# Layer 2's latent branch with its gates and z projections spread one by one, its merge set up two steps later, and the last column's squares summed by TensorE

## The chip, the cores and the metric

The program runs on one NeuronCore of a Trainium2 chip. The core has five engines with queues of their own: TensorE (PE; its weight loads are shown as PEld), VectorE (DVE), ScalarE (ACT), GpSimd (POOL) and SyncE (SP), which here issues every DMA. The metric is the device time of one execution in microseconds. The kernel before took 2572.04 us, the median of three runs from 2567.85 to 2572.58 us.

## The reference: what is computed

Two layers of a decoder trunk work on 16 meta tokens and 1024 tokens of width 1024. In each layer the tokens are normalised and multiplied by one wide matrix. Its columns feed three token mixers (forgetting attention, "FoX"; latent attention, "MLA"; sliding-window attention, "SWA"), one gate path z of 512 columns for each, and three times 1024 merge gates:

```python
h = rmsnorm(x, norm_g)
proj = h @ w_in          # a_q a_k a_v a_f a_z | b_cq b_ckv b_kr b_z | c_q c_k c_v c_z | gates
branches = stack([y_a * silu(a_z), y_b * silu(b_z), y_c * silu(c_z)])
proj_br = einsum('blnw,nwd->blnd', branches, w_branch)
merged = sum(sigmoid(gates) * proj_br, over the three branches)
x = x + merged @ w_out
```

A last rmsnorm closes the program, and the meta tokens are dropped. A norm needs, for each token, the sum of the squares of its 1024 values.

## The kernel before

**Tiles.** Channels lie on partitions, so a normalised input is a pair of tiles hh and hl of 128 partitions by 8 by 1040 tokens: each float32 is split into a rounded high part and the rest (split, L154). A product is then three matmuls, high by high, low by high and high by low (mm3, L171, with its three matmuls in L175 to L177). Tokens are taken in chunks: qch is two chunks of 512 in layer 2 and 264, 264 and 512 in layer 1; the last stage of layer 2 takes four of 256.

**Order of the stages in a layer.** Values and projections, then the three branches one after the other (FoX, SWA, MLA), then the merge (L1014 to L1023: for each branch n_, load_y and eight calls of branch), then the output columns with the next norm (L1026 to L1079).

**Fillers.** The attention of a head is a chain through four engines: scores on PE (L1002), a minimum on DVE (L255), an exponential on ACT (L260), transposes on PE (L268), a split by ACT and DVE (L157, L158), products with v (L310, L312). Other work stands between the groups of a head. The table PLAN (L61) has for each layer three lists, for FoX, SWA and MLA. Its entries are called in order by fill() (L737): one ahead of the branch, and one after each group of four query blocks. MLA in layer 2 has eight heads of two groups each, so 17 entries. The letters mean:

- g: gate(), L652: one of the layer's 24 merge gates is projected (8 steps of mm3 for each of two chunks, 48 matmuls), copied out by ACT (L657) and stored to gate_d;
- z: one of the branch's four z projections, also 48 matmuls, with a tanh on ACT (L734) and a product on DVE (L735) into a tile zs, of which there are two buffers; the z of head pair j is used up by POOL in L355;
- r: merge_starts(), L914: the layer's normalised input is given up (no projection may follow), its memory becomes acc and the tiles of the merge, and load_y(0) brings FoX's y from DRAM pair by pair through one buffer yt, which POOL rounds and subtracts (L936, L938);
- s: branch(0, d), L942: one of FoX's eight products with w_branch, 24 matmuls, and its gate's tanh (L952) and product (L956). What the plan leaves of the eight is done after the attention by L1022.

All fillers use the PSUM tag pj, of two banks, and the weight buffers wr, wh and wl, of two each. A weight tile is 512 KB: one DMA, a cast on ACT (L157) and a subtraction on POOL (L158).

**finish and finish_late.** After a pair of heads finish() (L322) sends the reciprocal sums through DRAM; at the end of every fill() finish_late() (L343) scales the oldest waiting pair: two products on POOL (L354 by the sums, L355 by z) and the store to y_d.

**What sets the order on an engine.** The code is traced in program order, but the program is made with schedule_with_timeline_sim=True (L1171): a planner that models the time of each instruction sets the order on each engine's queue when the program is built, within what data and buffers allow. The code's order is its priority, not the order that runs. Each queue is then served in that order.

**The norm's sum of squares.** column() (L1041) makes one of eight output columns of a chunk: mm3, the addition to x (L1044), and add_square() (L216), where ACT squares (L221) and POOL adds to the running tile sq (L222); for the last column DVE does that addition. rstd() (L187) then multiplies a matrix of ones by sq (L192), which adds over the partitions, and makes the reciprocal root (L199 to L204). This matmul is in plain float32 and appears as two records in the profile. In layer 1 the norm feeds layer 2 (normed, L207); in layer 2 it feeds the output (L1066 to L1079).

Of the kernel before, what the change touches and what calls it, by code (L numbers as in the profile page):

```python
# [11 lines left out]
F32 = mybir.dt.float32  # L12
F32R = mybir.dt.float32r
AF = mybir.ActivationFunctionType
# [4 lines left out]
P = 128  # L19
D = 1024  # L20
KD = D // P
# [42 lines left out]
     "g g . z g z g . g g zzr s . . sss s s".split()),  # L64
    ("g z . . z . g . . gg z . z g gg . gg".split(),
     "gg zg z g . gg zz g gg".split(),
     "g gg . z . z g . . g zzr . ss . ss s s".split()),
)


def _f(ap):
    return ap.bitcast(F32)
# [13 lines left out]
def tile_kernel(ctx: ExitStack, tc, a, out):  # L86
    nc = tc.nc
# [9 lines left out]
    def psum(tag):  # L97
        return ps.tile([P, 512], F32, tag=tag, name=f"ps_{tag}", bufs=PSB[tag])

    def dma(dst, src):  # L100
        nc.sync.dma_start(*(_f(x) if x.dtype == F32R else x for x in (dst, src)))
# [5 lines left out]
    def dense():  # L107

        turn[0] += 1
        return psum(banks[0][turn[0] % len(banks[0])])  # L110
# [18 lines left out]
    ones = const.tile([P, P], F32, tag="ones", name="ones")  # L129
# [24 lines left out]
    def split(hi, lo, src, scale=None, eng=None):  # L154

        if scale is None:
            nc.scalar.copy(hi, src)  # L157
            (eng or nc.vector).tensor_tensor(lo, src, _f(hi), ALU.subtract)  # L158
        else:
            nc.scalar.activation(hi, src, AF.Copy, scale=scale)  # L160
            nc.vector.scalar_tensor_tensor(lo, src, scale, _f(hi), ALU.mult, ALU.subtract)

    def weights(src, n):
        raw = wp.tile([P, 1024], F32, tag="wr", name="wr", bufs=2)
        dma(raw[:, :n], src)
        wh = wp.tile([P, 1024], F32R, tag="wh", name="wh")
        wl = wp.tile([P, 1024], F32R, tag="wl", name="wl")
        split(wh[:, :n], wl[:, :n], raw[:, :n], eng=nc.gpsimd)
        return wh, wl

    def mm3(dst, wh, wl, rh, rl, nk, m, c0, c1):  # L171

        for k in range(nk):
            w1 = wh[:, k * P:k * P + m]
            nc.tensor.matmul(dst, w1, rh[:, k, c0:c1], start=(k == 0), stop=False)  # L175
            nc.tensor.matmul(dst, w1, rl[:, k, c0:c1], start=False, stop=False)  # L176
            nc.tensor.matmul(dst, wl[:, k * P:k * P + m], rh[:, k, c0:c1],  # L177
                             start=False, stop=(k == nk - 1))
# [5 lines left out]
            mm3(t[:m, :c1 - c0], wh, wl, rh, rl, nk, m, c0, c1)  # L184
            evac(t[:, :c1 - c0], c0, c1)

    def rstd(pool, sq, c0, c1, dim, parts=None):  # L187

        n = c1 - c0
        v = psum("t")[:, :n]  # L190
        if parts is None:
            nc.tensor.matmul(v, ones, sq[:, c0:c1], start=True, stop=True)  # L192
        else:
            for k in range(parts):
                t = pool.tile([P, 512], F32, tag="sqt", name="sqt", bufs=4)[:, :n]
                nc.scalar.activation(t, sq(k)[:, c0:c1], AF.Square)
                nc.tensor.matmul(v, ones, t, start=(k == 0), stop=(k == parts - 1))
        r = pool.tile([P, 512], F32, tag="rs_r", name="rs_r", bufs=1)[:, :n]
        nc.scalar.activation(r, v, AF.Ln, bias=epsc, scale=1.0 / dim)  # L199
        nc.scalar.activation(r, r, AF.Exp, scale=-0.5)  # L200
        nc.vector.tensor_scalar(v, v, -0.5 / dim, -0.5 * EPS, ALU.mult, ALU.add)
        nc.vector.tensor_tensor(v, v, r, ALU.mult)
        nc.vector.tensor_tensor(v, v, r, ALU.mult)
        nc.vector.scalar_tensor_tensor(v, v, 1.5, r, ALU.add, ALU.mult)  # L204
        return v

    def normed(pool, xk, nk, sq, chunk, dim, gc, hh, hl, parts=None):  # L207
        c0, c1 = chunk
        r = rstd(pool, sq, c0, c1, dim, parts)
        for k in range(nk):  # L210
            h = psum("o")[:, :c1 - c0]
            nc.vector.scalar_tensor_tensor(h, xk(k)[:, c0:c1], gcol[:, gc + k:gc + k + 1], r,
                                           ALU.mult, ALU.mult)
            split(hh[:, k, c0:c1], hl[:, k, c0:c1], h)

    def add_square(pool, sq, x, c0, c1, first, eng, sqb=1):  # L216
        if first:
            nc.scalar.activation(sq[:, c0:c1], x, AF.Square)
        else:
            t = pool.tile([P, 512], F32, tag="sqt", name="sqt", bufs=sqb)[:, :c1 - c0]  # L220
            nc.scalar.activation(t, x, AF.Square)  # L221
            eng.tensor_tensor(sq[:, c0:c1], sq[:, c0:c1], t, ALU.add)  # L222
# [257 lines left out]
    def table(name):  # L480
        tc.keep_in_program_order(nc.scalar.preload_act_table_set(f"{name}_and_others"))
# [5 lines left out]
    hh = hpool.tile([P, KD, L], F32R, tag="hh", name="hh")  # L487
    hl = hpool.tile([P, KD, L], F32R, tag="hl", name="hl")
    va = tc.alloc_tile_pool(name="va0", bufs=1, side=B, reuse_waits="tile")
    banks[0] = MOST  # L490
    with tc.tile_pool(name="s0", bufs=4, side=A, reuse_waits="tile") as s0:
        x0 = s0.tile([P, KD, L], F32, tag="x0", name="x0", bufs=1)
        sq = s0.tile([P, L], F32, tag="sq", name="sq", bufs=1)
# [17 lines left out]
        for c0, c1 in START:  # L511
            xk = lambda k: x0[:, k]
# [9 lines left out]
    for l in range(DEPTH):  # L522
# [80 lines left out]
        with tc.tile_pool(name=f"wq{l}", bufs=2, side=B, reuse_waits="tile") as pw:  # L603
# [20 lines left out]
            for kv in range(2):  # L624
                ws = [weights(w1[T_CQ + 2 * kv + i], 1024) for i in range(2)]
                rows = [row_pair(pw) for _ in range(2)]
                for c0, c1 in qch:
                    n = c1 - c0
                    xs = []
                    for i in range(2):  # L630
                        t = dense()[:, :n]
# [44 lines left out]
        with tc.tile_pool(name=f"lr{l}", bufs=2, side=B, reuse_waits="tile") as pr:  # L676
            for t0, nk, dim, gc, dh, dl, chunks in (
# [3 lines left out]
                sq = pr.tile([P, L], F32, tag="sq", name="sq")  # L681
# [8 lines left out]
        with tc.tile_pool(name=f"mq{l}", bufs=2, side=A, reuse_waits="tile") as pm:  # L690
            values(vb, 1, ws, 2, cvh, cvl, between=some)
            wh, wl = weights(a["wkn"][l], 1024)
            for pair in range(4):
                rows = row_pair(pm)
                for c0, c1 in FULL:
                    t = dense()[:, :c1 - c0]
# [10 lines left out]
            for part in (2, 0, 1):  # L707
                wh, wl = weights(a["wuq"][l, part], 768)
                rows = [row_pair(pm) for _ in range(2)]
                for c0, c1 in qch:  # L710
                    n = c1 - c0
                    xs = []
                    for i in range(2):
                        t = dense()[:, :n]
# [107 lines left out]
        with tc.tile_pool(name=f"swk{l}", bufs=2, side=A, reuse_waits="tile") as pk, \  # L822
# [12 lines left out]
            for kv in range(2):  # L835
# [14 lines left out]
                for i in range(-1 if first else 0, NB):  # L850
# [11 lines left out]
                    for jj in range(2):  # L862
                        t = psum("s").rearrange("p (j c) -> p j c", j=2)
                        for j2 in range(2):
# [3 lines left out]
                                             start=True, stop=False)  # L868
                            nc.tensor.matmul(dst, ql[j][:, q0:q0 + rows], kc[:, k0:k0 + nk_],
                                             start=False, stop=True)  # L870
# [17 lines left out]
                    parts = [(0, NM, 0)] if i < 0 else [(0, P, i), (P, P, i + 1)]  # L888
                    for pi, (kcol0, kk, blk) in enumerate(parts):
# [3 lines left out]
                                         start=(pi == 0), stop=False)  # L893
                        nc.tensor.matmul(o[:, :width], vc[:kk, blk, kv, :], pl[:kk, :width],
                                         start=False, stop=(pi == len(parts) - 1))
# [134 lines left out]
        xn = xp.tile([P, KD, L], F32, tag="xn", name="xn")  # L1030
        if first:
            hpool = tc.alloc_tile_pool(name=f"h{l + 1}", bufs=1, side=A, reuse_waits="tile")
            hh = hpool.tile([P, KD, L], F32R, tag="hh", name="hh")
            hl = hpool.tile([P, KD, L], F32R, tag="hl", name="hl")
            vw = tc.alloc_tile_pool(name=f"vw{l}", bufs=1, side=A, reuse_waits="tile")
        with tc.tile_pool(name=f"so{l}", bufs=2, side=B, reuse_waits="tile") as po:
            sq = po.tile([P, L], F32, tag="sq", name="sq", bufs=1)
            for d in range(KD):
                dma(xn[:, d, lo:], (a["xT"] if first else x_d)[d][:, lo:])

            def column(d, w, c0, c1):  # L1041
                t = dense()[:, :c1 - c0]
                mm3(t, w[0], w[1], mt[c0][0], mt[c0][1], KD, P, 0, c1 - c0)
                nc.vector.tensor_tensor(xn[:, d, c0:c1], t, xn[:, d, c0:c1], ALU.add)  # L1044
                add_square(po, sq, xn[:, d, c0:c1], c0, c1, d == 0,
                           nc.vector if d == KD - 1 else nc.gpsimd, 2)
                if first:
                    dma(x_d[d, :, c0:c1], xn[:, d, c0:c1])

            for d in range(KD - 2):  # L1050
                w = weights(a["wo"][l, d], 1024)
                for c0, c1 in och:
                    column(d, w, c0, c1)
                if first and d == 2:
                    early_ws = value_weights(vw, [a["wv0"][l + 1]], KD)
            last = [(d, weights(a["wo"][l, d], 1024)) for d in (KD - 2, KD - 1)]
            banks[0] = MOST
            for c0, c1 in och:
                for d, w in last:
                    column(d, w, c0, c1)  # L1060
                if c0 == lo:
                    table("natural_log_exp")
                if first:
                    normed(po, lambda k: xn[:, k], KD, sq, (c0, c1), D, 8, hh, hl)
                else:
                    r = rstd(po, sq, c0, c1, D)  # L1066
                    rb = po.tile([P, 512], F32, tag="rb", name="rb")[:, :c1 - c0]
                    nc.scalar.copy(rb, r)
                    for k in range(KD):
                        h = xn[:, k, c0:c1]  # L1070
                        g = gcol[:, 16 + k:17 + k]
                        if k in (1, 4, 6):
                            nc.scalar.activation(h, h, AF.Copy, scale=g)
                            nc.gpsimd.tensor_tensor(h, h, rb, ALU.mult)
                        else:
                            nc.vector.scalar_tensor_tensor(h, h, g, r, ALU.mult, ALU.mult)
                        if k % 2:
                            dma(out.rearrange("k p n -> p k n")[:, k - 1:k + 1, c0 - NM:c1 - NM],
                                xn[:, k - 1:k + 1, c0:c1])  # L1079
# [6 lines left out]
            sq=3240, sk=3752, sv=3880, sz=4008, g=4520)  # L1086
# [89 lines left out]
```

## Time and profile before

| | |
|---|---|
| median of three runs | 2572.04 us (2567.85 to 2572.58) |
| the profiled execution | 2568.92 us, of which the span from its first to its last instruction is 2567.0 us |
| mean granted TensorE clock | 0.995 |
| layer 2's latent branch | from about 2093 (the first scores) to 2370 us of the span |
| layer 2's merge, rest of it | to about 2460 us |
| output columns and last norm | to 2567 us |

A row of a timeline gives the start in us from the span's start, the duration, the engine, the line, the operation, out<-in by the program's names, the shapes and how many were joined; in brackets stands the idle time before it and what ended it. Matmuls are pipelined: their ends are modelled, and the time that one costs in a dense row of them is the distance from start to start. A table by stretches gives for each engine the busy time and the number of instructions, then PE's granted clock, the busy share of the DMA engines and GB/s.

### The profile page before, as it was taken

How to read it: one execution, taken by the hardware profiler on the slowest of the kernel's cores; microseconds unless marked ns; L12 is line 12 of the kernel's file. 1: busy time of each engine (PE TensorE's matmuls, PEld its weight loads, DVE VectorE, ACT ScalarE, POOL GpSimd, SP SyncE). 2: the span in 40 equal slices, each digit the busy share in tenths (PEclk: the TensorE clock that was granted, in tenths of full speed). 3: DMA queues.
4: the chain of work that ended last, by engine and by line, in shares of the span. 5: the costliest groups of instructions: out<-in, count | busy, mean ns of one | idle time of the engine just before them, and what ended most of it. 6: DMA issues, size and time to landing. Idle time of an engine off the chain costs nothing.

```text
span 2567.0 us, 42088 instructions
## 1 busy us (share of the span) xinstructions
PE 2518.8 (98%) x15446; PEld 2252.2 (88%) x15446; DVE 1286.1 (50%) x3286; ACT 1206.4 (47%) x2704; POOL 1003.7 (39%) x983
## 2 busy tenths in 40 slices
PE   8999999999999999999999999999999999999998
PEld 7999899999888999999998888888887888888897
DVE  5464355544363445677156453545434623566743
ACT  5233355545374456654233343555445634566433
POOL 4141545344332424453523325445323342352544
PEclk9999999999999999999999999999999999999999
DMA  5144512222634434364323354121216362453532
GB/s 170 56 140 149 193 55 82 73 76 77 175 105 111 134 96 125 101 227 172 112 92 89 108 191 145 67 83 59 87 71 178 103 173 75 122 146 118 190 128 74
DMA packets 137630, 303.39 MB, mean 118 GB/s; under 512 B 22560, under 2 KB 63296, under 8 KB 137424
## 3 DMA queue, kind: packets, MB, share of 16 engines
q1 hardware_dynamic: 137424, 300.71, 37.2%
q8 instruction: 122, 2.00, 0.3%
q14 instruction: 84, 0.69, 0.1%
HBM read 211.98 MB, written 88.66 MB: 117 GB/s over the span
## 4 chain that ended last, share of the span: by engine, by line
PE 87%; DMA 5%; DVE 3%; ACT 2%; POOL 2%; issue 1%; SPq 1%; POOLq 0%; ACTq 0%; DVEq 0%
PE ps_pj L177 15%; PE ps_pj L176 15%; PE ps_pj L175 15%; PE ps_t L268 6%; PE ps_s L1002 3%; PE ps_o L312 3%; PE ps_s L176 3%; PE ps_s L177 3%; PE ps_s L175 3%; PE ps_o L310 2%; PE ps_t L177 1%; PE ps_t L176 1%; PE ps_o L176 1%; PE ps_t L175 1%; PE ps_s L804 1%; PE ps_s L802 1%
## 5 line engine op out<-in xcount | busy, mean ns | idle before, releaser
L175 PE MATMUL ps_pj<-hh,wh 128*128 128x512 f32 (+1 forms) x1920 | 673.2, 351 | 4.2 <-ACT gt L657 2.0
L158 POOL TENSOR_TENSOR wl<-wr,wh 128x1024 fp32r<-128x1024 f32 (+1 forms) x156 | 376.5, 2414 | 766.2 <-ACT wh L157 644.0
L177 PE MATMUL ps_pj<-hh,wl 128*128 128x512 f32 (+1 forms) x1920 | 670.1, 349 | 2.2 <-POOL wl L158 2.2
L176 PE MATMUL ps_pj<-hl,wh 128*128 128x512 f32 (+1 forms) x1920 | 671.5, 350 | 0.0
L175 PEld LDWEIGHTS ps_pj<-hh,wh 128*128 128x128 f32 x1920 | 361.8, 188 | 47.8 <-ACT gt L657 2.6
L177 PEld LDWEIGHTS ps_pj<-hh,wl 128*128 128x128 f32 x1920 | 362.1, 189 | 43.5 <-POOL wl L158 2.4
L176 PEld LDWEIGHTS ps_pj<-hl,wh 128*128 128x128 f32 x1920 | 361.9, 189 | 39.4 <-issue 0.5
L158 DVE TENSOR_TENSOR ptl<-ps_t,pth 128x512 fp32r<-128x512 f32 (+1 forms) x386 | 244.6, 640 | 143.1 <-ACT pth L157 137.3
L260 ACT ACTIVATE P<-P,mn 128x656 f32<-128x656 f32 (+8 forms) x272 | 207.0, 761 | 164.6 <-DVE mn L255 160.0
L157 ACT CAST pth<-ps_t 128x512 fp32r<-128x512 f32 (+1 forms) x386 | 205.8, 546 | 166.7 <-PE ps_t L268 134.7
L157 ACT CAST wh<-wr 128x1024 fp32r<-128x1024 f32 (+1 forms) x156 | 162.1, 1039 | 241.4 <-PE ps_pj L176 131.8
L268 PE MATMUL ps_t<-ident,P 128*128 128x128 f32 x1152 | 187.6, 276 | 0.8 <-DVE ptl L158 0.7
L310 PE MATMUL ps_o<-pth,vp 128*128 128x256 f32 (+1 forms) x640 | 167.5, 277 | 2.7 <-DVE u L281 1.8
L312 PE MATMUL ps_o<-ptl,vp 128*128 128x256 f32 (+1 forms) x640 | 159.5, 287 | 1.9 <-DVE ptl L158 1.7
L298 POOL COPY pmeta<-P 128x16 f32<-128x16 f32 x256 | 49.4, 196 | 271.2 <-ACT P L260 262.8
L1002 PE MATMUL ps_s<-kt,qt 96*128 96x328 f32 (+9 forms) x696 | 147.3, 329 | 2.7 <-DVE mn L255 2.7
L268 PEld LDWEIGHTS ps_t<-ident,P 128*128 128x128 f32 x1152 | 135.1, 141 | 8.9 <-DVE ptl L158 1.5
L310 PEld LDWEIGHTS ps_o<-pth,vp 128*128 128x128 f32 x640 | 121.1, 189 | 11.0 <-issue 1.7
L809 POOL TENSOR_TENSOR cm<-ckb,tri 128x128 f32<-128x128 f32 (+1 forms) x136 | 60.3, 445 | 176.4 <-DVE mn L255 172.6
L312 PEld LDWEIGHTS ps_o<-ptl,vp 128*128 128x128 f32 x640 | 120.8, 189 | 8.3 <-DVE ptl L158 4.4
L281 DVE TENSOR_TENSOR u<-ps_o,hv 64x256 f32<-64x256 f32 x128 | 53.9, 421 | 135.9 <-ACT hv L280 120.9
L1002 PEld LDWEIGHTS ps_s<-kt,qt 96*128 96x128 f32 (+1 forms) x696 | 108.9, 188 | 10.0 <-DVE mn L255 5.2
(357 smaller groups left out, 5647.3 us busy)
## 6 DMA issues: line engine op xcount, KB each, us to landing
wr<-in_w_dram SPq DMA_DIRECT2D x108, 512.0 KB
gate_d<-gt SPq DMA_DIRECT2D x72, 256.0 KB
gt<-gate_d SPq DMA_DIRECT2D x24, 520.0 KB
wr<-in_wbr_dram SPq DMA_DIRECT2D x24, 512.0 KB
gt<-gate_d SPq DMA_DIRECT2D x24, 512.0 KB
kn_d<-sg SPq DMA_DIRECT2D x16, 520.0 KB
ckb<-ck_d SPq DMA_DIRECT2D x16, 520.0 KB
kt<-kn_d SPq DMA_DIRECT2D x16, 520.0 KB
```

The costliest lines, as they stand in the source:

```text
L157: nc.scalar.copy(hi, src)
L158: (eng or nc.vector).tensor_tensor(lo, src, _f(hi), ALU.subtract)
L175: nc.tensor.matmul(dst, w1, rh[:, k, c0:c1], start=(k == 0), stop=False)
L176: nc.tensor.matmul(dst, w1, rl[:, k, c0:c1], start=False, stop=False)
L177: nc.tensor.matmul(dst, wl[:, k * P:k * P + m], rh[:, k, c0:c1], start=False, stop=(k == nk - 1))
L260: nc.scalar.activation(s[:rows, :n], s[:rows, :n], AF.Exp, bias=prev, scale=-1.0, accum_out=total)
L268: nc.tensor.transpose(t[:kk, c:c + rows], src, ident[:rows, :rows])
L281: nc.vector.tensor_tensor(u[mine, :n], o[mine, :n], t[mine, :n], ALU.add)
L310: nc.tensor.matmul(dst, vp[:, j + x, vs], ph[:, cols], start=(j + x == 0), stop=False)
L312: nc.tensor.matmul(dst, vp[:, j + x, vs], pl[:, cols], start=False, stop=(diag and x == 1))
L809: nc.gpsimd.tensor_tensor(cm[:rows, :rows], ckb[:rows, d:n], tri[:rows, :rows], ALU.add)
L1002: nc.tensor.matmul(dst, q[:, qi, q0:q0 + rows], kt[:, ki, c0:c1], start=(x == 0), stop=(x == 2))
```

## The change

Two edits that have nothing to do with each other in the code.

The third list of layer 2's plan:

```diff
-     "g gg . z . z g . . g zzr . ss . ss s s".split()),
+     "g g . z . z g . g . zg . zr . ss ss s".split()),
```

Both have 17 entries, five g, four z and one r. The second g of the second entry moves: the gates stand in entries 1, 2, 7, 9 and 11 instead of 1, 2, 2, 7 and 10. The third z stays in entry 11 and the fourth goes from entry 11 to entry 13, and r with it. The plan has five s instead of six, in entries 15, 15, 16, 16 and 17 instead of 13, 13, 15, 15, 16 and 17; so three of the eight products of FoX's merge are left for the loop after the attention, instead of two.

The squares of the last column, in both layers:

```diff
-    def rstd(pool, sq, c0, c1, dim, parts=None):
+    def rstd(pool, sq, c0, c1, dim, parts=None, more=None):
...
-            nc.tensor.matmul(v, ones, sq[:, c0:c1], start=True, stop=True)
+            nc.tensor.matmul(v, ones, sq[:, c0:c1], start=True, stop=more is None)
+            if more is not None:
+                nc.tensor.matmul(v, ones, more, start=False, stop=True)
...
-                add_square(po, sq, xn[:, d, c0:c1], c0, c1, d == 0,
-                           nc.vector if d == KD - 1 else nc.gpsimd, 2)
+                if d == KD - 1:
+                    t = po.tile([P, 512], F32, tag="sqt", name="sqt", bufs=2)[:, :c1 - c0]
+                    nc.scalar.activation(t, xn[:, d, c0:c1], AF.Square)
+                else:
+                    add_square(po, sq, xn[:, d, c0:c1], c0, c1, d == 0, nc.gpsimd, 2)
                 if first:
                     dma(x_d[d, :, c0:c1], xn[:, d, c0:c1])
+                return t
```

The squares of the last column are no longer added to sq. They stay in their own tile, column() returns it, and a second matmul with the ones adds them in PSUM to the sum that the first one makes of sq. The calls of normed() and rstd() pass the tile on as more.

More of the change, by code (lines that the diff above doesn't have):

```diff
@@ L205, in rstd, with normed @@
         return v
-    def normed(pool, xk, nk, sq, chunk, dim, gc, hh, hl, parts=None):
+    def normed(pool, xk, nk, sq, chunk, dim, gc, hh, hl, parts=None, more=None):
         c0, c1 = chunk
-        r = rstd(pool, sq, c0, c1, dim, parts)
+        r = rstd(pool, sq, c0, c1, dim, parts, more)
         for k in range(nk):
@@ L1059, in tile_kernel @@
                 for d, w in last:
-                    column(d, w, c0, c1)
+                    more = column(d, w, c0, c1)
                 if c0 == lo:
@@ L1063, in tile_kernel @@
                 if first:
-                    normed(po, lambda k: xn[:, k], KD, sq, (c0, c1), D, 8, hh, hl)
+                    normed(po, lambda k: xn[:, k], KD, sq, (c0, c1), D, 8, hh, hl, more=more)
                 else:
-                    r = rstd(po, sq, c0, c1, D)
+                    r = rstd(po, sq, c0, c1, D, more=more)
                     rb = po.tile([P, 512], F32, tag="rb", name="rb")[:, :c1 - c0]
```

## The prediction

> **What bounds the kernel now.** I read the page's busy shares first, then tables of busy time by stretch over layer 2's latent branch, then timelines at the places that they point to.
>
> ```profile
> span 2567.0 us, 42088 instructions
> PE 2518.8 (98%) x15446; PEld 2252.2 (88%) x15446; DVE 1286.1 (50%) x3286; ACT 1206.4 (47%) x2704; POOL 1003.7 (39%) x983
> ```
>
> TensorE is busy for 98% of the span. So a matmul more costs its full length wherever TensorE is full, and a rearrangement can win only idle time, 2567.0 - 2518.8 = 48.2 us in the whole program. The question is how much of that lies where the plan of layer 2's latent branch is edited. The stretches, with time, then busy time of PE, weight load, DVE, ACT and POOL, then the granted clock:
>
> ```profile
> core 0: us, PE busy (x) PEld busy (x) DVE busy (x) ACT busy (x) POOL busy (x), PEclk, DMA share, GB/s
> 2205.00:2222.00 17.00, 15.84 (x102) 14.24 (x101) 12.70 (x35) 12.95 (x29) 8.25 (x10) 0.90 0.41 89
> 2222.00:2238.00 16.00, 15.83 (x85) 13.46 (x84) 6.55 (x17) 4.90 (x11) 0.20 (x1) 1.00 0.17 56
> 2238.00:2284.00 46.00, 43.47 (x296) 38.34 (x295) 37.07 (x104) 36.60 (x80) 36.93 (x40) 1.00 0.68 184
> ...
> 2340.00:2372.00 32.00, 27.65 (x168) 23.24 (x167) 22.15 (x48) 20.26 (x42) 3.38 (x7) 1.00 0.32 109
> ```
>
> TensorE idles 17.00 - 15.84 = 1.16 us, 2.53 us and 4.35 us in three of them. I call them hole A, hole B and the end. The same table for the instructions that touch hh alone (the projections: two of three of their matmuls read it) says what the holes are:
>
> ```profile
> 2205.00:2222.00 17.00, 1.05 (x3) 0.38 (x2) 0.00 (x0) 0.00 (x0) 0.00 (x0) 0.90 0.41 89
> 2222.00:2238.00 16.00, 10.28 (x32) 6.02 (x32) 0.00 (x0) 0.00 (x0) 0.00 (x0) 1.00 0.17 56
> 2238.00:2284.00 46.00, 0.00 (x0) 0.00 (x0) 0.00 (x0) 0.00 (x0) 0.00 (x0) 1.00 0.68 184
> ```
>
> In A and B there is next to no projection to put between the attention's matmuls; all of the fourth z (32 of its 48 matmuls read hh) runs between them. What opens and closes the holes is seen in the timelines of POOL and DVE:
>
> ```profile
> 2219.30 2.40 POOL L355 TENSOR_TENSOR u<-u,zs 128x1024 f32<-128x1024 f32 x1
> ...
> 2241.34 2.95 POOL L936 TENSOR_SCALAR y<-yt 128x512 fp32r<-128x512 f32 x2
> ...
> 2280.86 2.55 POOL L938 TENSOR_TENSOR y<-yt,y 128x512 fp32r<-128x512 f32 x2
> ```
> ```profile
> 2221.73 1.28 DVE L735 SCALAR_TENSOR_TENSOR zs<-ez,ps_pj 128x512 f32<-128x512 f32 x2 [0.38 <-POOL u L355]
> ...
> 2279.01 1.28 DVE L735 SCALAR_TENSOR_TENSOR zs<-ez,ps_pj 128x512 f32<-128x512 f32 x2
> ```
>
> There are two zs buffers. The third z is multiplied but can't leave its two pj banks until POOL has used pair 0's z (L355 at 2219.30): hole A. The fourth z, multiplied by 2238, waits in the same way for pair 1's, until 2279.01. Once its matmuls are done, the layer's input is freed, the merge gets its memory, and POOL splits y from 2241.34 to 2283.4; only then has branch() operands: hole B. So the letters of the plan do not set where projections run. They run ahead, in their own order, until a buffer stops them. That decides how I price the edit.
>
> **The change, part by part.** *Order of the projections.* Before, the stream of the branch is g, g, g, z, z, g, g, z, z and then branches; after, it is g, g, z, z, g, g, z, g, z. The one real move is a gate from before the first z to between the third and the fourth. A dense projection's pitch is that of this row of the chain that ended last (start, us, what):
>
> ```profile
> 2163.66 0.23 PE ps_pj L176
> ```
>
> 48 matmuls by 0.23 us are 11.0 us for a gate, 24 by 0.23 are 5.5 us for a branch(). With the gate go its weight load and two stores on SP, ACT's cast and two copies, and POOL's 2.4 us split. All pass the loads of keys and queries on SP, and I price them at nothing: PE waits for no load in these stretches, and without the lead that those loads have one late load would cost its own few us.
>
> Before the third z there are 11.0 us less to fill with, so that z gets stuck earlier. While projections are plentiful they take some two thirds of PE (the fourth z's 11.0 us lie within 16); without them the attention speeds up, so pair 0 ends earlier too, and I let hole A grow by 8 us, not 11. Its idle rate is 1.16 / 17 = 0.07 us per us, so +0.5 us. Bounds: 0, if pair 0 ends 11 us earlier, and 2.2, with one more loss of the clock:
>
> ```profile
> 2205.00:2213.00 8.00, 6.86 (x45) 5.83 (x43) 5.49 (x16) 6.47 (x13) 2.77 (x3) 1.00 0.01 3
> 2213.00:2217.00 4.00, 3.98 (x18) 3.41 (x19) 3.55 (x10) 3.18 (x9) 0.51 (x2) 0.63 0.86 181
> ```
>
> Within hole A the granted clock is 0.63 over 4 us: half speed for 3.0 us of them, and the 0.90 of the whole 17 us makes it 17 x 0.10 x 2 = 3.4 us, a loss of 1.7 us. It came after 8 us in which PE idled 1.14 us in all. [...]
>
> *Hole B.* It runs from the last matmul of the fourth z to the end of the y split, and both ends move together. The gate that now fills after the third z shortens nothing of it; r two fills later could lengthen it, were it bound by its letter, which the trace denies. I take 0, between -2.5 (its idle gone) and +1.1 (20 us more at 2.53 / 46 = 0.055). Twenty us is a head: the exponentials of hole B are
>
> ```profile
> 2238.00:2284.00 46.00, 16.02 (x36) 1.00 0.68 184
> ```
>
> 36 records, two for each of 18 softmaxes; 8 make a head, 20.4 us.
>
> *The end.* One branch() moves from the plan to the dense loop behind it: 5.5 us more that PE can put into the end. The waits of PE there are
>
> ```profile
> PE ps_o L371 <- ACT pm L369: 1.5, 1, 1.5
> PE ps_s L175 <- ACT y L934: 1.0, 1, 1.0
> PE ps_s L176 <- POOL y L938: 0.8, 1, 0.8
> ```
>
> The last two are waits for the second branch's y, which that work can cover: -1.8 us, with -3.3 (all three) and 0 (it has run before them) as bounds. Its gate tile comes from the second pool instead of the first; I price that at nothing, since the load is issued well ahead.
>
> *Squares.* Seven DVE additions (three chunks in layer 1, four in layer 2) go, and seven matmuls on ones come. Their cost on a full PE, at 256 and at 512 columns:
>
> ```profile
> 2541.75 0.59 PE L192 MATMUL ps_t<-sq,ones 128*128 128x256 f32 x2
> 2541.99 0.47 PE L176 MATMUL ps_s<-m,wh 128*128 128x256 f32 x1
> 2542.29 0.28 PE L177 MATMUL ps_s<-m,wl 128*128 128x256 f32 x1
> 2542.41 0.28 PE L175 MATMUL ps_s<-m,wh 128*128 128x256 f32 x1
> ```
> ```profile
> 1301.41 1.02 PE L192 MATMUL ps_t<-sq,ones 128*128 128x512 f32 x2
> 1301.87 0.71 PE L456 MATMUL ps_s<-wvh,hl 128*128 128x320 f32 x1
> 1302.42 0.31 PE L454 MATMUL ps_pj<-wvh,hh 128*128 128x320 f32 x1
> 1302.56 0.31 PE L455 MATMUL ps_pj<-wvl,hh 128*128 128x320 f32 x1
> ```
>
> From 2541.75 to 2542.29 lie one such matmul and a plain one, whose pitch is 0.12: 0.54 - 0.12 = 0.42 us. At 512 columns it is 1.01 - 0.14 = 0.87 us. Layer 1 has chunks of 264, 264 and 512: 0.43 + 0.43 + 0.87 = 1.7 us. The first three chunks of layer 2 cost 3 x 0.42 = 1.3 us. Nothing hides these: PE is full there, and the additions that go were hidden behind it. Only the last chunk has the addition in its chain:
>
> ```profile
> 2554.00 0.40 ACT L221 ACTIVATE sqt<-xn 128x256 f32<-128x256 f32 x1
> 2554.39 0.43 DVE L202 TENSOR_TENSOR ps_t<-ps_t,rs_r 128x256 f32<-128x256 f32 x1
> 2554.74 0.41 DVE L222 TENSOR_TENSOR sq<-sq,sqt 128x256 f32<-128x256 f32 x1
> 2555.07 0.42 DVE L203 TENSOR_TENSOR ps_t<-ps_t,rs_r 128x256 f32<-128x256 f32 x1
> 2555.21 0.70 PE L192 MATMUL ps_t<-sq,ones 128*128 128x256 f32 x2 [1.72 <-DVE sq L222]
> ```
>
> The matmul on sq moves into PE's idle 1.72 us, the one on the squares can start at 2554.4 instead of 2555.21. But DVE has the chunk before it in hand and serves both in turn, so what reaches the end is the slot of L222 there, 2555.07 - 2554.74 = 0.3 us. I take -0.3, between 0 and -1.6 (the 0.8 us of PE's earlier start twice, should the third chunk gain it too). New is a wait on ACT: the last column's square stays in one of two buffers until its matmul has read it, so ACT's square of the next chunk may wait, with that chunk's evacuations behind it. PE's columns cover that in all chunks but the last, which has no successor.
>
> Sum: 1.7 + 1.3 - 0.3 + 0.5 + 0 - 1.8 = +1.4 us. The profiled execution took 2568.92 us, 1.9 us more than its span, and would take 2570.3. The median of the runs shown is 2572.04, 3.1 above it, which I carry over: 2573.4 us. The bounds of the terms together, -4.4 and +6.3, give 2568 to 2578. A measurement of this kernel can tell about 0.2%, 5.1 us, from no change.
>
> **The rivals.** *The holes close.* If the late gate and the late branch reach all the idle time, 1.16 + 2.53 + 4.35 us go, and with the clock drop 1.7 more: -9.7, and with the squares' +2.7 it is -7.0: 2565.0 us. For it speaks that 11.0 us of projection now lie just ahead of B; against it, that B is set by the y split, 42 us of it on POOL.
>
> *The merge really comes late.* If the two fills hold back the load of y by a head, hole B grows by 20.4 us, the clock falls once more (1.7), and the price per us decides: 0.055 as in B, or that of the end's first part, where nothing at all fills:
>
> ```profile
> 2355.00:2364.00 9.00, 6.68 (x43) 5.10 (x42) 4.82 (x9) 5.72 (x13) 0.00 (x0) 1.00 0.31 98
> ```
>
> 2.32 / 9 = 0.26. At that price it is 1.4 + 1.7 + 5.3 = +8.4: 2580.4 us. It turns the forecast into slower from 0.10 us per us on. For it: single buffers of yt, and loads of later heads queued behind them on SP. Against it: before, the merge ran well ahead of its letter.
>
> *The plan does nothing.* If the projections end up where they were, the squares' +2.7 remain: 2574.7 us.
>
> *No clock drop.* If hole A no longer has the pattern of idling that costs the clock, the sum is 1.7 lower: 2571.7 us. One drop in a trace can be chance. [...]
>
> **How the numbers follow.** Forecast 0.43, holes close 0.21, merge late 0.21, plan without effect 0.10, no drop 0.05. All but the second and third lie within 5.1 us: same 0.58, faster 0.21, slower 0.21. The three runs shown spread over 4.7 us, so 2 us go below the first rival and 0.6 above the second: 2563 to 2581. The forecast's own range is 2568 to 2578.
>
> **What would show it.** Right: fillers in the order above; hole A longer by some 8 us and B near 46; the two waits for y at the end gone; L192's neighbour with the new matmul 0.42 to 0.87 us longer in each chunk; no DVE addition of squares. Wrong: the y split starting more than 10 us after the fourth z's last matmul, TensorE idling more than 12 us between the gates and the second branch, or layer 1 changed by more than its 1.7 us.

## The result and the profile after

| | before | after |
|---|---|---|
| median | 2570.12 us (20 runs, 2566.27 to 2573.57) | 2573.78 us (20 runs, 2568.75 to 2579.39) |
| the profiled execution | 2568.92 us, span 2567.0 | 2569.45 us, span 2567.6 |

The ratio of after to before is 1.0016, with a 95% interval of 1.0009 to 1.0022: 0.0016 x 2570 = 4.1 us slower. That is within the 0.2% that the prediction called no change, and 2573.8 us lies beside the forecast of 2573.4. But the forecast set +1.4 us on a base of 2572.04; with twenty runs that base came out 1.9 us lower, and the change cost 2.7 us more than the sum said. The two nearly cancel, so it is luck that the number came so close. The question is which terms were short. The profiled execution of after is the second lowest of its 20 runs, so the spans of single profiles settle nothing here. All runs below were fast but one of 2742.24 us, of the kernel before with one s less, which its ratio leaves out.

In the changed kernel the lines behind L192 have numbers two higher, up to L1044 (before's L952 is L954). The head of its page:

```profile
span 2567.6 us, 42109 instructions
PE 2521.4 (98%) x15460; PEld 2253.0 (88%) x15460; DVE 1284.1 (50%) x3279; ACT 1207.3 (47%) x2704; POOL 1004.2 (39%) x983
```

There are 14 matmul records more (seven matmuls of two records), 7 DVE instructions less, and PE is busy 2.6 us longer. The table by stretches (time, busy PE, weight load, DVE, ACT and POOL, granted clock), with the bounds moved to where the holes now lie:

```profile
2195.00:2212.00 17.00, 15.63 (x106) 13.68 (x105) 12.82 (x36) 13.52 (x29) 8.19 (x10) 1.00 0.46 113
2212.00:2242.00 30.00, 30.00 (x165) 26.04 (x164) 11.72 (x31) 11.12 (x22) 8.10 (x6) 1.00 0.21 69
2242.00:2287.00 45.00, 41.08 (x271) 36.26 (x270) 30.82 (x87) 31.52 (x70) 31.29 (x35) 1.00 0.62 176
...
2340.00:2372.00 32.00, 29.38 (x163) 24.27 (x161) 20.17 (x45) 19.73 (x38) 5.03 (x7) 0.95 0.35 116
```

Hole A idles 17.00 - 15.63 = 1.4 us (1.2 before), hole B 3.9 us (2.5 before), the end 2.6 us (4.4 before); but the end now has a granted clock of 0.95. What opens and closes the holes is as it was. The timelines of POOL and DVE:

```profile
2208.12 2.39 POOL L357 TENSOR_TENSOR u<-u,zs 128x1024 f32<-128x1024 f32 x1
...
2249.12 2.94 POOL L938 TENSOR_SCALAR y<-yt 128x512 fp32r<-128x512 f32 x2 [0.98 <-DMA yt<-y_d]
...
2285.84 1.29 POOL L940 TENSOR_TENSOR y<-yt,y 128x512 fp32r<-128x512 f32 x1
```
```profile
2210.89 1.27 DVE L737 SCALAR_TENSOR_TENSOR zs<-ez,ps_pj 128x512 f32<-128x512 f32 x2
2272.67 1.27 DVE L737 SCALAR_TENSOR_TENSOR zs<-ez,ps_pj 128x512 f32<-128x512 f32 x2
```

The third z leaves its banks behind pair 0's L357, and the merge's products can begin only when the last split of y has ended at 2287.1, 42 us after the last matmul of a projection, which ended at 2244.7.

**What had not been foreseen lies at the end.** The products of FoX's merge leave their banks by DVE. In before, the rows of the two chunks of the first product that the plan leaves to the tail (d = 6), then of the first chunk of the last (d = 7):

```profile
2338.37 0.69 DVE L956 SCALAR_TENSOR_TENSOR acc<-gt,ps_pj 128x512 f32<-128x512 f32 x1 [1.30 <-PE ps_pj L177]
2352.12 0.69 DVE L956 SCALAR_TENSOR_TENSOR acc<-gt,ps_s 128x512 f32<-128x512 f32 x1 [0.34 <-PE ps_s L177]
2365.59 0.69 DVE L956 SCALAR_TENSOR_TENSOR acc<-gt,ps_t 128x512 f32<-128x512 f32 x1 [2.14 <-PE ps_t L177]
```

In after, one product more is left to the tail, and between the plan's last one and the tail's first no product leaves its banks for 40 us:

```profile
2326.64 0.68 DVE L958 SCALAR_TENSOR_TENSOR acc<-gt,ps_pj 128x512 f32<-128x512 f32 x1
2366.65 0.69 DVE L958 SCALAR_TENSOR_TENSOR acc<-gt,ps_s 128x512 f32<-128x512 f32 x1 [3.15 <-ACT gt L954]
```

That first product waits for a gate, not for PE. The reason stands in one line of branch(): an odd d takes its gate tile from the second pool, gp2, as soon as there is one, and gp2 gets its memory when the last pair of heads has given up fin. With two products in the tail, the first is d = 6 and takes its tile from the first pool; with three it is d = 5, which is odd. Its load is issued at 2360.95, and the loads of y for the next branch stand behind it and the gate of d = 7. SP's timeline of before, then of after:

```profile
2360.56 0.34 SPq L101 DMA_DIRECT2D gt<-gate_d  x1
2361.07 1.09 SPq L101 DMA_DIRECT2D rb<-rt_d  x2
2362.25 1.01 SPq L101 DMA_DIRECT2D yt<-y_d  x2
```
```profile
2360.95 0.54 SPq L101 DMA_DIRECT2D gt<-gate_d  x1
2361.58 0.45 SPq L101 DMA_DIRECT2D rb<-rt_d  x1
2362.09 0.58 SPq L101 DMA_DIRECT2D gt<-gate_d  x1
2362.76 0.85 SPq L101 DMA_DIRECT2D yt<-y_d  x2
```

On ACT the first copy of y (L936) then stands behind the tanh of those gates, and the tanh waits for the gate loads:

```profile
2365.98 1.16 ACT L954 ACTIVATE gt<-gt 128x512 f32<-128x512 f32 x2 [3.31 <-DMA gt<-gate_d]
2368.11 1.16 ACT L954 ACTIVATE gt<-gt 128x512 f32<-128x512 f32 x2 [0.97 <-DMA gt<-gate_d]
2369.39 1.14 ACT L936 CAST y<-yt 128x512 fp32r<-128x512 f32 x2
```

### The profile page after: what moved, and what is told of

Read it like the earlier page. It is cut to its first block, busy times and chain, and to the rows that moved or that the text cites. A ratio compares the mean times of both kernels' runs of the same rounds, so it can differ in the third digit from the quotient of the medians.

```text
span 2567.6 us, 42109 instructions
## 1 busy us (share of the span) xinstructions
PE 2521.4 (98%) x15460; PEld 2253.0 (88%) x15460; DVE 1284.1 (50%) x3279; ACT 1207.3 (47%) x2704; POOL 1004.2 (39%) x983
## 4 chain that ended last, share of the span: by engine, by line
PE 78%; DMA 5%; DVE 4%; ACT 2%; issue 1%; POOL 1%; SPq 1%; POOLq 0%; ACTq 0%; DVEq 0%
PE ps_pj L175 14%; PE ps_pj L176 14%; PE ps_pj L177 14%; PE ps_t L270 5%; PE ps_s L1004 3%; PE ps_o L314 3%; PE ps_o L312 2%; PE ps_s L177 2%; PE ps_s L175 2%; PE ps_s L176 2%; PE ps_s L806 1%; PE ps_s L804 1%; PE ps_o L177 1%; PE ps_o L176 1%; PE ps_o L175 1%
```

## The experiments

The first four kernels ran on one chip, the next four on a second, the last four on a third, each with its own runs of the kernel before; medians are compared within a chip. The ratio is not the quotient of the two medians; the two differ by up to 0.0004 (the control, the sixth row, has 0.9989 by its medians).

| kernel | median us (before on the same chip) | ratio | 95% interval |
|---|---|---|---|
| squares alone | 2570.09 (2568.75) | 1.0006 | 0.9998 to 1.0015 |
| plan alone | 2572.58 (2568.75) | 1.0013 | 1.0004 to 1.0022 |
| the change again | 2575.03 (2568.75) | 1.0024 | 1.0011 to 1.0038 |
| squares, seven sums more | 2592.19 (2568.75) | 1.0097 | 1.0081 to 1.0112 |
| plan, gate tile from the first pool | 2570.34 (2569.03) | 1.0003 | 0.9994 to 1.0012 |
| before, gate tile from the first pool | 2566.11 (2569.03) | 0.9993 | 0.9984 to 1.0001 |
| before with gate and merge moved | 2570.19 (2569.03) | 1.0006 | 0.9997 to 1.0015 |
| before with one s less | 2572.58 (2569.03) | 1.0015 | 1.0006 to 1.0023 |
| plan, y loaded first | 2571.91 (2568.69) | 1.0009 | 0.9999 to 1.0020 |
| before, both tail gates in the second pool | 2570.46 (2568.69) | 1.0006 | 0.9997 to 1.0015 |
| the change, gate tile from the first pool | 2571.43 (2568.69) | 1.0014 | 1.0005 to 1.0023 |
| a version meant to be faster | 2568.16 (2568.69) | 0.9998 | 0.9989 to 1.0007 |

### The halves

The squares' edit on the old plan, the new plan with the old squares, and both once more on this chip.

> The kernel before with the second edit alone: the last column's squares go to TensorE. Theory A (added matmuls cost their full length where TensorE is full): +2.7 us, ratio 1.0010, with 0.42 to 0.87 us more on TensorE in each of six chunks. Theory B (the plan is what costs): no change, within 1 us, since DVE's additions go. Theory C (the time lies in losses of TensorE's clock, which differ from run to run): the ratio follows the mean granted clock, about 1.3 us for each 0.0005 of it.

> The kernel before with the first edit alone: the third list of layer 2's plan. Theory A: the plan's part of the sum, -1.3 us, ratio 0.9995, anywhere from -7 to +4 by its bounds. Theory B: +3 to +4 us, ratio 1.0013, nearly the whole of the change. Theory C: as the mean granted clock says; lower than before's if it is slower.

> The changed kernel itself beside the two halves, on the same chip. All theories: ratio 1.0009 to 1.0022. If the halves add, it is the product of their ratios.

The halves give 1.0006 and 1.0013, together 1.0019, between the 1.0016 and the 1.0024 of the whole; the 1.0024 of six runs lies above the range expected. The larger half is the plan, which I had put at -1.3 us (0.5 - 1.8): theory B had its 1.0013, and theory A's 0.9995 lies outside the interval. The squares' 1.0006 lies between A and B. Theory C does not hold for them: their mean granted clock was 0.9970, above before's 0.9960 on this chip, and they were not faster. In the plan's trace TensorE's waits near the end are

```profile
PE ps_t L175 <- ACT y L934: 3.8, 1, 3.8
PE ps_o L371 <- ACT pm L369: 1.5, 1, 1.5
PE ps_t L176 <- POOL y L938: 0.5, 1, 0.5
```

So the wait for y that I had going away, 1.0 us of ACT and 0.8 of POOL before, has grown to 4.3 us.

### The price of a sum by ones

The squares' edit, with seven products of the ones with a zero tile between the two that it has:

```diff
             if more is not None:
+                z = pool.tile([P, 512], F32, tag="zeros", name="zeros", bufs=1)[:, :n]
+                nc.gpsimd.memset(z, 0.0)
+                for _ in range(7):
+                    nc.tensor.matmul(v, ones, z, start=False, stop=False)
                 nc.tensor.matmul(v, ones, more, start=False, stop=True)
```

> The squares edit alone, with seven more matmuls of the ones with a tile of zeros in each of the seven chunks of the two norms (they add nothing to the result; POOL clears the tile each time). Theory A: 2.7 + 7 x (1.7 + 1.3 + 0.42) = +26.6 us, ratio 1.0103. Theory B, with matmuls that find idle time: less than half of that, +13 us or less.

Between this kernel and the squares alone lie 2592.19 - 2570.09 = 22.1 us, 3.2 us for each set of seven sums. My prices add up to 1.7 + 4 x 0.42 = 3.4 us a set. On a full PE they hold, and theory A's 1.0103 lies within the interval.

### The gate tile

One line in branch(), on the plan alone and, as a control, on the kernel before:

```diff
-            gr = (gp2 if gp2 and d % 2 else gp).tile([P, L], F32, tag="gt", name="gt", bufs=2)
+            gr = (gp2 if n_ and d % 2 else gp).tile([P, L], F32, tag="gt", name="gt", bufs=2)
```

> The plan edit alone, and one more line: FoX's tail products take their gate tile from the first pool, where it is free, instead of from the second pool, which is allocated only when the last heads of the attention have been released. Theory G (the gate tile: the first tail product is d = 5, its gate load is issued only at 2360.95 us in the changed kernel's trace, and its psum bank, those of d = 6 and d = 7 behind it and two gate loads wait for that): the cost of the plan, 1.0013, goes; ratio 0.9998 to 1.0004, and the first tail product is read out near 2335 us instead of near 2367. Theory O (the order of the stretch from 2205 to 2287 us, the merge late, costs the time): ratio stays 1.0010 to 1.0016. Theory C (only the number of clock drops in a run): the ratio goes with the mean granted clock, whatever the tile.

> The kernel before with the same one line on the gate tile: the control. Theory G: in the kernel before only the last of the two tail products, d = 7, waits for the second pool, so little is gained, ratio 0.9995 to 1.0000. Theory O and theory C: 1.0000 within what the measurement can tell.

The plan's 1.0013 becomes 1.0003, as theory G said, though on another chip; the control's 0.9993 is a little more than theory G's 0.9995 allowed, with an interval that takes in 1. The intervals of each pair overlap, and the line acts in layer 1 too: there the time from the last scores to FoX's last product grew by 0.6 to 1.1 us and that of the output columns fell by about 1. By theory C the plan with the line should have stayed as slow, since its mean clock is that of the plan alone, 0.9953. The traces are plainer. The first tail product of the plan with this line is read out at 2334.38 us, where theory G had 2335 (2369.32 in the plan alone). SP and ACT of the control:

```profile
2360.11 0.34 SPq L101 DMA_DIRECT2D yt<-y_d  x1
2360.61 2.40 SPq L101 DMA_DIRECT2D rb<-rt_d  x2
2363.07 0.58 SPq L101 DMA_DIRECT2D yt<-y_d  x1
2363.75 0.84 SPq L101 DMA_DIRECT2D gt<-gate_d  x2
```
```profile
2364.64 1.14 ACT L934 CAST y<-yt 128x512 fp32r<-128x512 f32 x2 [2.31 <-DMA yt<-y_d]
```

No gate load stands just before y any more, the first copy of y starts at 2364.64 (2368.85 in before, 2369.39 in after), and no wait of PE for y is left in either kernel. With the new plan two others appear, though; the waits near the end of the plan with this line:

```profile
PE ps_o L371 <- ACT pm L369: 1.6, 1, 1.6
PE ps_o L310 <- DVE u L281: 1.0, 1, 1.0
PE ps_t L364 <- ACT rt L333: 0.6, 1, 0.6
```

The tail's products now run, and are read out, beside the last steps of the attention, and ACT comes to these later (its first copy of pm, L367, starts at 2364.36 instead of 2361.08); that this is why TensorE waits is argued, not tried. So 1.6 of the 4.3 us came back.

### Order, and one product less

The kernel before with two other plans. The first moves the gate and the merge as the change does and keeps six s; the second takes out the last s and nothing else:

```diff
-     "g gg . z . z g . . g zzr . ss . ss s s".split()),
+     "g g . z . z g . g . zg . zr . ss ss ss".split()),
```
```diff
-     "g gg . z . z g . . g zzr . ss . ss s s".split()),
+     "g gg . z . z g . . g zzr . ss . ss s .".split()),
```

> The kernel before with the gate and the merge moved as in the change, but with its own six projection steps inside the attention, so that the tail begins with d = 6 as before, whose gate tile is in the first pool. Theory G: no cost beyond hole A's and B's, ratio 0.9997 to 1.0005. Theory O: 1.0010 to 1.0016, as the plan edit alone has it.

> The kernel before with its gates, z and merge where they are, and only the last projection step taken out of the plan, so that it falls into the tail, as the change has it. Theory G: the plan's whole cost, ratio 1.0008 to 1.0016, with the first tail product's gate load issued near 2361 us and its readout near 2367. Theory O: 0.9993 to 1.0002 (what my prediction gave the end: 1.8 us less).

One s less has all that the plan costs, 1.0015, with every gate, z and merge where it was; its first tail product is read out at 2367.96 us. Its waits near the end are

```profile
PE ps_t L175 <- ACT y L934: 2.3, 1, 2.3
PE ps_o L371 <- ACT pm L369: 1.5, 1, 1.5
PE ps_t L176 <- POOL y L938: 0.5, 1, 0.5
```

The order alone gives 1.0006, from 0.9997 to 1.0015, between what the two theories expected: by its time neither no cost nor the plan's can be shut out. Its trace has the waits for y of before, 1.0 and 0.8 us.

### The queue, and both tail gates late

First the new plan with the odd gate tile left where it is, but with two y loads issued as soon as gp2 exists:

```diff
         gp2 = tc.alloc_tile_pool(name=f"gg{l}", bufs=1, side=A, reuse_waits="tile")
+        for pair in range(2):
+            yt = gp2.tile([P, L], F32, tag="yt", name="yt", bufs=2)
+            dma(yt[:, lo:], y_d[2, pair, :, lo:])
+            pre.append(yt)
...
-                yt = (gp2 if n_ else gp).tile([P, L], F32, tag="yt", name="yt", bufs=2 if n_ else 1)
-                dma(yt[:, lo:], y_d[n_, pair, :, lo:])
+                yt = pre.pop(0) if n_ and pre else None
+                if yt is None:
+                    yt = (gp2 if n_ else gp).tile([P, L], F32, tag="yt", name="yt", bufs=2 if n_ else 1)
+                    dma(yt[:, lo:], y_d[n_, pair, :, lo:])
```

> The plan edit alone, with the gate tiles left in the second pool as in the change, but the first two y loads of the next branch issued as soon as the second pool is allocated, ahead of the gate loads of the tail products. Theory Q (the cost of the plan is the order on SP's queue: two gate loads stand before the y loads, and TensorE waits for y): the plan's 1.0013 falls to 0.9996 to 1.0006, though the first tail product is still read out only near 2367 us. Theory H (the cost is the psum banks held and the product steps that fill nothing between 2330 and 2366 us): the ratio stays at 1.0010 to 1.0016.

Its 1.0009, from 0.9999 to 1.0020, does not tell Q from H. In its trace the copies of y now come ahead of the gates on ACT, and TensorE's waits for y shrink from 4.3 us to 0.3 for ACT and 0.9 for POOL:

```profile
PE ps_o L176 <- POOL y L941: 0.9, 1, 0.9
PE ps_o L175 <- DVE acc L959: 0.5, 1, 0.5
PE ps_t L175 <- ACT y L937: 0.3, 1, 0.3
```

So the order of the loads does make the wait. Whether that is the whole cost stays open.

Then the kernel before with its own plan, and the gate tiles of both tail products in the second pool:

```diff
-            gr = (gp2 if gp2 and d % 2 else gp).tile([P, L], F32, tag="gt", name="gt", bufs=2)
+            gr = (gp2 if gp2 and (d % 2 or n_ == 0) else gp).tile([P, L], F32, tag="gt", name="gt", bufs=2)
```

> The kernel before with its plan untouched, and both tail products, d = 6 and d = 7, given their gate tiles in the second pool: the change's fault put in on purpose. Theory G, in either form: slower by the plan's cost or near it, 1.0006 to 1.0016, with two gate loads issued near 2361 us ahead of the y loads. Theory O (order of gates, z and merge): 1.0000 within what the measurement can tell, since the plan is that of before.

The time, 1.0006, is at the lower edge of what G said, and its interval takes in 1. The trace has the fault: two gate loads ahead of y on SP, and 1.8 us of waiting for y in one piece.

```profile
2359.23 0.86 SPq L101 DMA_DIRECT2D gt<-gate_d  x1
2360.18 0.45 SPq L101 DMA_DIRECT2D rb<-rt_d  x1
2360.69 0.58 SPq L101 DMA_DIRECT2D gt<-gate_d  x1
2361.36 0.88 SPq L101 DMA_DIRECT2D yt<-y_d  x2
```
```profile
PE ps_s L175 <- ACT y L934: 1.8, 1, 1.8
```

That is the 1.8 us that before had in two waits. With two products in the tail, a late first gate makes the waits for y no longer than they were; with three they are 1.0 us in after, 2.3 in its repeat, 2.8 with one s less and 4.3 in the plan alone.

### The change mended, and a version meant to be faster

The whole change with the gate tile's line; and the plan of before with that line and the squares' edit in layer 2's last chunk only (column() keeps the square apart only `if d == KD - 1 and not first and c0 == och[-1][0]`, and adds on DVE otherwise).

> The whole change with the tail products' gate tiles taken from the first pool. Theory G: the change's 1.0016 loses what the plan alone lost with this line (1.0013 to 1.0003), so 1.0003 to 1.0010, what is left being the squares. Theory O: 1.0013 to 1.0022 as the change has it.

> The plan of before, the gate tiles of the tail products from the first pool, and the squares summed by TensorE only in layer 2's last chunk, where no other work covers the addition (my own price for that chunk: 0.3 us less, bounds 0 to 1.6 less). Theory G with that price: 0.9985 to 0.9994 (0.9993 for the gate tile by its own run, less 0.0001 to 0.0006). If the gate tile's 0.9993 was noise: 0.9994 to 1.0000.

Both missed what theory G said. The mended change has 1.0014 where it had 1.0003 to 1.0010; that lies in theory O's range, and the interval reaches down to 1.0005. So the gate tile is not shown to be the plan's whole cost. The version meant to be faster has 0.9998, from 0.9989 to 1.0007, in the range for the case that the control's gain was noise: the 0.9993 of the gate tile's line did not come again, and no run here shows a kernel faster than before by more than the interval.

### All runs together

Single ratios are too coarse for terms of one or two microseconds, so I fitted the times of before, of after and of nine of these kernels (all but the seven sums more, y first and the last version; 224 runs) as a mean for each chip plus a fixed number for each part that a kernel has. It gives the squares +1.8 us (1.1 either way at 95%), gate and merge moved +1.7 (1.0), a tail whose first gate is late +2.0 (0.9), and the gate tile's line -1.2 (1.2). It assumes that parts add: those of the change make 5.5 us, where its two measurements gave 4.1 and 6.2. By it the order costs about as much as the late gate.

The clock that the runs were granted differs with them. Its mean is 0.9954 over the 103 runs of the nine kernels with another plan or with both tail gates in the second pool (the change and its repeat among them), and 0.9961 over the 90 runs of before on the three chips: 0.0007 x 2568 = 1.8 us, if TensorE pays for it in full. One drop to half for 3.4 us, as after's profile has it from 2362.3 to 2365.7, counts 3.4 x 0.5 = 1.7 us in the same way, so that is one drop more in each run. It may not pay in full: within the runs of one kernel 0.001 of clock went with 1.2 us (0.3 either way, 230 runs), which makes it 0.8 us. The windows from 2340 to 2385 us show where: in before, the control, the plan with the gate tile's line and the mended change, each with its granted clock as the third number from the right:

```profile
2340.00:2385.00 45.00, 40.65 (x224) 33.86 (x223) 27.61 (x51) 25.87 (x51) 10.32 (x11) 1.00 0.44 152
```
```profile
2340.00:2385.00 45.00, 42.54 (x234) 36.01 (x233) 30.20 (x55) 27.92 (x53) 12.86 (x13) 1.00 0.46 153
```
```profile
2340.00:2385.00 45.00, 41.57 (x227) 35.24 (x226) 27.27 (x51) 26.82 (x50) 11.36 (x10) 0.96 0.48 163
```
```profile
2340.00:2385.00 45.00, 41.41 (x229) 35.32 (x228) 27.90 (x54) 26.31 (x50) 10.81 (x11) 0.92 0.40 134
```

45 x 0.04 is 1.8 us, one drop, and 0.92 is two. Of the seven kernels with three products in the tail six have a drop there, of the other seven profiles one (both gates late). In these profiles this goes with the third product, and the gate tile's line doesn't undo it, which may be why the mended change was not mended in full. In the 3.4 us just before the first such drop TensorE was busy for only 1.1 to 1.8 us in all seven (1.67 in after). In the plan alone, the repeat, one s less and both gates late, the wait for y lies in that stretch; in after, the plan with the line and the mended change it is the attention's last waits. So in those four a late gate may have cost twice, by a wait of 1.8 to 4.3 us and by the half clock behind it, 3.4 us of it for each drop.

Counted from the first scores of the latent branch to the first output column, TensorE loses 3.4 us to half clock (half of the time spent at it) and idles 9.1 us in the mean of the seven profiles with three products, and 1.0 and 8.2 us in the other seven. Of the 3.3 us between them 2.4 are clock. But that is one profile for each kernel. Over all runs the order alone and both gates late, with two products in the tail, have mean clocks of 0.9956 and 0.9955, hardly above the 0.9953 of the seven with three. What brings the drop is argued from these profiles and was not tried by itself.

## Why the number was right and a term was not

**The step that failed** is the sentence on the moved product: "Its gate tile comes from the second pool instead of the first; I price that at nothing, since the load is issued well ahead." It can't be issued ahead of the pool's own memory, and that is the last thing that the attention frees: in the plan alone the load is issued at 2361.84 us, and with the tile from the first pool the product has been read out 27 us before that. I had seen the tile move and not asked when its pool begins. So the end's term was not -1.8 us with bounds of -3.3 and 0, but about +0.8 in the mean of four profiles (-0.8 to +2.5), without the clock: PE's waits for y there are 1.0 us in after's own profile, 4.3, 2.3 and 2.8 us in the plan alone, the repeat and one s less, against 1.8 us in before, and the fit puts the late gate at +2.0. One s less shows that the moved product alone is enough to make the kernel slower. How much of that is the gate's load is not shown: with the tile from the first pool the waits for y go, as I had thought that they would, but others of 1.6 us come, and the whole change with that line stayed at 1.0014.

**Holes.** Hole A was to idle 0.5 us more and hole B as before. From 2190 to 2295 us the profiles with a full clock there idle 105 - 100.60 = 4.4 us with the old order (the control) and 105 - 99.79 = 5.2 us with the new (the mended change):

```profile
2190.00:2295.00 105.00, 100.60 (x630) 88.01 (x629) 66.87 (x184) 64.06 (x139) 52.93 (x59) 1.00 0.52 134
```
```profile
2190.00:2295.00 105.00, 99.79 (x615) 87.65 (x614) 60.82 (x169) 61.59 (x130) 49.80 (x54) 1.00 0.46 128
```

Together +0.8 us for +0.5: the size was right, but it lies in B, not in A, which stayed 17 us of little filling instead of growing by 8. Neither rival came: the holes did not close, and the merge was not a head later: 42 us lie between the last projection and the y split's end in after, 46 before. What more the order may cost (+1.7 by the fit, where I had +0.5) is not traced.

**Squares.** The price of a sum on a full PE holds by the seven further ones. The last chunk was mis-sized: I took -0.3, for the slot of one DVE addition, and had -1.6 as the bound "should the third chunk gain it too". From the start of the last column matmul to the end of the span it is 2567.0 - 2553.2 = 13.8 us in every profile with the old squares, and 12.1 us in all four with the plain edit (2567.6 - 2555.5 in after): -1.7. With the edit in the last chunk only it is 13.6 us: -0.2. So the chunk before it does count, probably because its addition stood in DVE's queue ahead of the last chunk's. In after, the two sums of the last chunk:

```profile
2555.70 0.70 PE L192 MATMUL ps_t<-sq,ones 128*128 128x256 f32 x2
...
2556.32 0.42 ACT L1049 ACTIVATE sqt<-xn 128x256 f32<-128x256 f32 x1 [0.94 <-DVE xn L1046]
...
2556.79 0.70 PE L194 MATMUL ps_t<-sqt,ones 128*128 128x256 f32 x2 [0.38 <-ACT sqt L1049]
```

PE's wait for DVE's addition, 1.72 us, has become one of 0.38 us for ACT's square. With my 1.7 + 1.3 us for the rest, the squares would cost 3.0 - 1.7 = 1.3 us, where I had 2.7. The medians of the squares alone differ by 2570.09 - 2568.75 = 1.3 us too, but at the higher clock named above, and the fit says 1.8.

By stages the rest was not 1.7 + 1.3. From the first addition of an output column in layer 1 to FoX's first scores in layer 2 it is 366.1 to 368.3 us in the nine profiles with the old squares there, and 368.4 to 371.9 in the four with the plain edit: +3.2 in the mean, about 1.0 of it idle TensorE. That layer 1 changes by more than its 1.7 us was one of my signs of being wrong. Layer 2's columns took 86.1 to 88.8 us, and 88.3 to 89.3 with the edit: +0.9. These add up to 3.2 + 0.9 - 1.7 = +2.4 us. Why layer 1 pays more stays open.

**Clock.** My sum leaves the clock as it was in before, with one drop in the stretch of hole A. In after's profile hole A has a clock of 1.00 and the drop is at the end. Hole A idled 1.4 us there, and 1.2 us in before at a clock of 0.90; that its idling costs the clock was my estimate, and no run shows it. Over all runs the granted clock says about one drop more than before, not the same number, so the clock is a second term that was too small, 0 against +0.8 to +1.7 us; the rival "no clock drop" pointed the wrong way.

**The sum anew**, from the traces: squares +1.3 to +2.4, holes +0.8, waits for y from 1.8 to 2.6 us in the mean of the four profiles with three tail products and a late tile whose y loads stand behind the gates (+0.8), the clock +0.8 to +1.7: +3.7 to +5.7 us, against 4.1 measured (6.2 in the repeat) and +1.4 forecast. The sum fits, but it does not say how much of the clock's part the late gate brings.

## What to carry to other kernels

When a step moves out of one loop into another, look up for each of its tiles which pool it comes from there, and when that pool gets its memory; a tile that was free in the old place can be the last thing freed in the new one. Then read who stands behind its load on the queue, and behind its first reader on that engine (here y, behind two gate loads and their tanh: 4.3 us of TensorE waiting in the plan alone, 1.2 us with y loaded first). And where an addition leaves an engine that serves two chunks in turn, its saving can count in the chunk before the last too: here 1.7 us, against 0.2 with the last chunk alone.

## What the runs showed of the hardware

In after's profile the clock fell to half at 2362.3 us, for 3.4 us. TensorE's longest wait in the 2.3 us before it was the 1.5 us for ACT's pm (L373). The stretch before the drop, then the drop itself (its 0.50 is the granted clock):

```profile
2360.00:2362.30 2.30, 0.75 (x7) 0.45 (x5) 1.71 (x3) 1.93 (x5) 0.00 (x0) 1.00 0.32 66
2362.30:2365.70 3.40, 3.40 (x9) 2.63 (x10) 0.69 (x1) 0.38 (x1) 0.00 (x0) 0.50 1.02 289
```

Before, the control and the order alone have the same wait of 1.5 us there and a clock of 1.00 from 2340 to 2385 us. In the two profiles of before and after, the drops between 100 and 2500 us start whole multiples of a drop's own 3.413 us apart: at 128.49, 1046.68 and 2214.03 us in before, which is 269 and 342 times that, and at 126.59 and 2362.32 us in after, 655 times that. In the 3.41 us just before each of two drops TensorE was busy for 1.67 us (after's at 2362.32) and for 2.25 us (before's at 2214.03). Two other stretches of that length, at whole multiples from those drops, have 1.99 us of work, from 2360.81 in before and from 2263.34 in after, and the clock stayed at 1.00 behind them. So the busy time of the 3.41 us ahead does not part these four, and what brings a drop is not shown.

A sum by ones of 256 columns in plain float32 took 0.42 us beside 0.12 for the kernel's own matmuls (before, 2541.75 to 2542.41 us), 3.5 times as long.
